# A hybrid decoder layer on one core: expert tiles in source order, and an overflow job's work in one place

## The chip, the cores and the metric

The kernel runs on 1 core of one Trainium2 chip. The metric is the device time of one execution in microseconds; the kernel before took 1674.36 us (median of 3 runs, 1674.21 to 1675.78).

## What is computed

One layer of a decoder with 1024 tokens of width 1024, in float32: a gated recurrence and an attention branch are merged into x, and then a mixture of experts is added. The change touches only the experts. Cut to that:

```python
def hier_moe(u, wg, bg, we, be, w1, w3, w2):          # 1024 tokens, 64 experts
    g_sel = argmax(u @ wg + bg)                       # one of 8 groups
    e_in_group = (u @ we + be)[group g_sel]           # 8 logits
    top_p, top_j = top_k(softmax(e_in_group), 2)      # two experts of that group
    gate = g_prob[g_sel] * top_p / sum(top_p)
    # each expert, on the tokens that chose it:
    h = silu(xb @ w1[e]) * (xb @ w3[e])               # 1024 -> 256
    y += gate * (h @ w2[e])                           # 256 -> 1024
x = x + hier_moe(rmsnorm(x), ...)
```

All 64 experts have tokens, so all their weights, 64 x 3 MiB, must pass through the core once.

## The kernel before

The first 1100 us compute projections, recurrence, attention and the merge; the change leaves them alone. Then comes **routing**: `product(tb)` and `route(tb)` (from L983 and L1006) make, for each of 8 blocks of 128 tokens, the merged x, write it to `xs_d` and to `out` in DRAM, choose the experts and give each of a token's two choices a place in a table in DRAM, `tab_d`, by an indirect transfer (L1154). A place belongs to a tile and a row: **32 tiles**, each of 128 rows, 64 rows for each of two experts. A choice that finds its expert's 64 rows full is left over and goes to a **job** of up to 64 rows of one expert. For tile 0 alone the row numbers are also made on the chip, by float32 products with a one-hot matrix (`first_tile`, L977), so that its rows can be fetched before the table is read back.

Then the **expert stage**. Its weights come in chunks of 1 MiB (`wchunk`, L1209): for a tile two chunks each of w1, w3 and w2 (`load`, L1272), six in all. There are `NW` = 19 chunk buffers, used in turn: five named c, four m (free from 973 us on) and ten w (free at 1095 us). All loads are issued by SP, in order, so a load whose buffer is still being read holds all loads behind it. For tile t the steps are

- `gather(t)`: GpSimd fetches the tile's rows from `xs_d` by an indirect DMA (L956) into one of six row tiles,
- `select(t)`: TensorE transposes the rows (L1263), VectorE scales them into xT (L1264),
- `gemm1(t)`: 64 products with w1 and w3 into ph (L1306); ScalarE and VectorE make hs of it (L1296, L1297),
- `turn(t)`: two transposes of hs (L1319), ScalarE copies them to hT (L1321),
- `gemm2(t)`: 16 products with w2 into py (L1333); VectorE adds them to the rows of `out` (L1336), which `gather_out(t)` has fetched into the same row tile (also L956),
- `scatter(t)`: GpSimd writes the rows back to `out` (L1253).

The loop (from L1471) writes gather(t+2), gather_out(t), the loads of tile t+2, gemm1(t), select(t+1), turn(t-1), gemm2(t-1), scatter(t-1). That order of the source is only a starting point: a scheduler sets the order on each engine by its own estimate. The job's rows are counted on the chip (`job_table`, `job_rec`), its chunks are loaded in the turn of tile `JI` = 6, its products (`job_run`: L1440, L1448, L1459) are split over the turns of tiles 8, 9 and 10, and its rows are fetched from `out` (L1416), added to (L1462) and written back (L1418). A loop at the end runs further jobs if there are any; in this execution there are none.

Of the kernel before, what the change touches and what calls it, by code (L numbers as in the profile page):

```python
# [38 lines left out]
NW = 19  # L39
# [4 lines left out]
JI = 6  # L44
# [7 lines left out]
def block_kernel(ctx, tc, x, positions, norm1_g, w_in, conv_w, conv_b, lru_wa, lru_ba, lru_wx,  # L52
# [878 lines left out]
    rec_0 = rt.tile([128, 4], F32, name="rec_0")  # L931
    tok_0 = rt.tile([128, 2], I32, name="tok_0")
    nc.gpsimd.memset(rec_0, 0.0)
    nc.gpsimd.memset(rec_0[:, 0:1], BIG)
    nc.gpsimd.memset(rec_0[:, 3:4], BIG)
    tokb = rt.tile([128, NB], F32, name="tokb")

    iota0 = rt.tile([128, 128], F32, name="iota0")
    nc.gpsimd.iota(iota0, pattern=[[NT_, 128]], base=0, channel_multiplier=0,
# [5 lines left out]
    nc.gpsimd.tensor_scalar(tokb, tokid, BIG, None, op0=ALU.add)  # L945
    nc.sync.dma_start(tab_d.rearrange("(p a) c -> p (a c)", p=128),
# [4 lines left out]
    nc.gpsimd.dma_start(g2c, norm2_g.rearrange("(k p) -> p k", p=128))  # L951
    blk = {}

    def rows_in(xg, at, src=xs_d):

        return nc.gpsimd.indirect_dma_start(  # L956
            out=xg, out_offset=None, in_=src,
            in_offset=bass.IndirectOffsetOnAxis(ap=at, axis=0),
            bounds_check=S - 1, oob_is_err=False)

    with pool_of(name="xe", bufs=1, side="right") as xe, \
# [15 lines left out]
        def first_tile(oh0, rec):  # L977

            for j in range(2):
                nc.tensor.matmul(pks[:, 128:132], oh0[:, j], rec[:, j], start=j == 0, stop=j == 1)  # L980
            nc.vector.tensor_tensor(rec_0, rec_0, pks[:, 128:132], op=ALU.add)
# [23 lines left out]
        def route(tb):  # L1005
            xt, ms, px = blk.pop(tb)  # L1006
            tsl = slice(tb * 128, tb * 128 + 128)
            if tb == NB - 1:
                blk["warm"] = xps.tile([128, D], F32, name="px")
                blk["xg"] = xgp.tile([128, D], F32, name="x2")  # L1010
                nc.gpsimd.memset(blk["xg"], 0.0)
# [80 lines left out]
            if tb:  # L1092
# [28 lines left out]
            oh0 = rp.tile([128, 2, 128], F32, name="oh0")  # L1121
            nc.vector.tensor_tensor(oh0, iota0[:, None, :].to_broadcast([128, 2, 128]),
                                    ps_[:, :, None].to_broadcast([128, 2, 128]), op=ALU.is_equal)
# [7 lines left out]
            rec0 = rp.tile([128, 2, 4], F32, name="rec0")  # L1131
            for c in (0, 3):
                nc.vector.tensor_scalar(rec0[:, :, c], rec[:, :, c], -BIG, None, op0=ALU.add)
# [6 lines left out]
            nc.vector.tensor_copy(rec0[:, :, 1:3], rec[:, :, 1:3])  # L1140
            if tb == NB - 1:
# [3 lines left out]
                warm(30, oh64)  # L1145
            blk["late"] = oh0, rec0
            if tb == 0:
                nc.vector.tensor_copy(acc, oh64)
            else:
                nc.vector.tensor_tensor(acc, acc, oh64, op=ALU.add)  # L1150
            for j in range(2):
# [7 lines left out]
                blk["tab"].append(sc)  # L1159

# [9 lines left out]
        for _ in route(NB - 1):  # L1170
# [9 lines left out]
    eg = open_pool(name="eg", bufs=1)  # L1180
    eh = open_pool(name="eh", bufs=2)
# [5 lines left out]
    onef = eg.tile([128, 64], F32, name="onef")  # L1187
    nc.gpsimd.memset(onef, 1.0)
    rec_all = eg.tile([128, NT_, 4], F32, name="rec_all")
    nc.gpsimd.dma_start(rec_all.rearrange("p a c -> p (a c)"),  # L1190
                      tab_d.rearrange("(p a) c -> p (a c)", p=128))
# [11 lines left out]
    def rec_of(t, c):  # L1203
        return rec_0[:, c:c + 1] if t == 0 else rec_all[:, t, c:c + 1]

    def tok_of(t, j=0):
        return tok_0[:, j:j + 1] if t == 0 else toki[:, j, t:t + 1]
# [11 lines left out]
    ring = {}  # L1219

    def rows_(kind):
        i = ring[kind] = ring.get(kind, -1) + 1
        if kind == "T":
            return xgp.tile([128, D], F32, name=f"x{3 + i % 2}")
# [326 lines left out]
```

## Time and profile before

| what | value |
|---|---|
| median of 3 runs | 1674.36 us |
| the profiled execution's own time | 1673.48 us |
| its span, first to last instruction | 1671.8 us |
| mean granted TensorE clock | 0.972 |
| TensorE busy | 1500.5 us, 90% |
| VectorE, ScalarE, GpSimd busy | 722.5, 498.8, 468.8 us |
| HBM read, written | 307.74 MB, 48.59 MB |

The page cuts the span into 40 slices of 41.8 us and gives each engine's busy share in tenths, the granted clock of TensorE, the busy share of the 16 DMA engines and the rate. The windows do the same for stretches that one chooses. A wait is put down to what ended it. PE is TensorE, DVE VectorE, ACT ScalarE, POOL GpSimd, SP the queue that issues the weight loads.

### The profile page before, as it was taken

The page shows a single profiled execution, that of the slowest core. Times are in us where ns is not written, and L with a number is a line of the kernel's source. Part 1 is how long each engine was busy: PE and PEld are TensorE (multiplying, and loading weights), DVE is VectorE, ACT ScalarE, POOL GpSimd, SP SyncE. Part 2 cuts the span into 40 slices and gives each one's busy share as a digit, 9 for nine tenths or more (in the row PEclk, how much of TensorE's full clock was granted, in tenths as well). Part 3 has the DMA queues.
Part 4 walks back from the last instruction along what each step waited for, and adds up shares of the span by engine and source line. Part 5 has one row for each costly group of instructions (what it writes and reads, how often), then busy time and mean ns, then how long its engine had stood idle before and what let it go on. Part 6 is the DMA issues. An engine that isn't in the chain of part 4 may idle for free. (4 is left out here: it accounts for less than half of the span.)

```text
span 1671.8 us, 22382 instructions
## 1 busy us (share of the span) xinstructions
PE 1500.5 (90%) x8484; PEld 1145.1 (68%) x8484; DVE 722.5 (43%) x1863; ACT 498.8 (30%) x1088; POOL 468.8 (28%) x467
## 2 busy tenths in 40 slices
PE   5999998999999989999898999979698698878876
PEld 5978886788888878888787877866354355444443
DVE  7744646320001687777885346754121122112111
ACT  5225464631111376666663112210000000000000
POOL 4034343322212245252703421132221212211100
PEclk9999999999999999999999999979899899999999
DMA  5212222353245110110206673387996999999995
GB/s 192 64 51 66 59 65 63 99 191 101 90 150 173 64 39 17 35 39 10 76 32 205 199 264 134 132 313 311 417 417 253 398 418 417 417 414 413 413 412 219
DMA packets 129665, 327.72 MB, mean 196 GB/s; under 512 B 17367, under 2 KB 82337, under 8 KB 105108
## 3 DMA queue, kind: packets, MB, share of 16 engines
q1 hardware_dynamic: 111684, 295.57, 47.3%
q0 software_dynamic: 14848, 21.46, 3.6%
q10 hardware_dynamic: 3024, 9.24, 1.4%
q8 instruction: 68, 1.11, 0.3%
q14 instruction: 41, 0.34, 0.1%
HBM read 307.74 MB, written 48.59 MB: 213 GB/s over the span
## 5 line engine op out<-in xcount | busy, mean ns | idle before, releaser
L116 POOL TENSOR_TENSOR w_lo<-w_raw,w_hi 128x1024 fp32r<-128x1024 f32 x40 | 97.8, 2444 | 263.0 <-ACT w_hi L113 263.0
L259 PE MATMUL pp<-uTh,w_hi 128*128 128x512 f32 x496 | 156.2, 396 | 1.1 <-ACT xp L368 1.1
L1264 DVE TENSOR_TENSOR x<-c,g2col 128x512 f32<-128x512 f32 (+1 forms) x66 | 44.3, 677 | 258.8 <-PE ph L1306 232.7
L262 PE MATMUL pp<-uTl,w_hi 128*128 128x512 f32 x496 | 156.1, 395 | 0.0
L1306 PE MATMUL ph<-w,x 128*64 128x256 f32 x992 | 138.9, 394 | 19.0 <-DMA w<-in_exp_w_dram 19.0
L265 PE MATMUL pp<-uTh,w_lo 128*128 128x512 f32 x496 | 155.7, 395 | 0.0
L1296 ACT ACTIVATE hs<-ph,rec_all 128x256 f32<-128x256 f32 x31 | 14.7, 473 | 440.0 <-PE ph L1306 440.0
L1306 PEld LDWEIGHTS ph<-w,x 128*64 128x64 f32 x992 | 83.6, 141 | 64.7 <-DMA w<-in_exp_w_dram 25.1
L259 PEld LDWEIGHTS pp<-uTh,w_hi 128*128 128x128 f32 x496 | 93.5, 189 | 23.3 <-ACT xp L368 1.1
L262 PEld LDWEIGHTS pp<-uTl,w_hi 128*128 128x128 f32 x496 | 93.6, 189 | 22.3
L265 PEld LDWEIGHTS pp<-uTh,w_lo 128*128 128x128 f32 x496 | 93.4, 188 | 22.1
L1002 PE MATMUL px<-wo,ms 128*128 128x512 f32 x384 | 95.0, 398 | 1.0 <-DVE ms L116 1.0
L1306 PE MATMUL ph<-c,x 128*64 128x256 f32 x592 | 85.2, 392 | 7.2 <-DMA c<-in_exp_w_dram 7.2
L113 ACT ACTIVATE w_hi<-w_raw 128x1024 fp32r<-128x1024 f32 x40 | 42.1, 1053 | 139.2 <-PE pp L262 112.8
L1002 PEld LDWEIGHTS px<-wo,ms 128*128 128x128 f32 x384 | 70.1, 188 | 16.9 <-issue 1.7
L1333 PE MATMUL py<-w,hT 128*64 128x512 f32 x280 | 76.3, 638 | 2.8 <-ACT hT L1321 1.6
L1306 PE MATMUL ph<-m,x 128*64 128x256 f32 x464 | 72.4, 394 | 6.3 <-DMA m<-in_exp_w_dram 6.3
L116 DVE TENSOR_TENSOR cTl<-gt,cTh 128x1024 fp32r<-128x1024 f32 x4 | 4.9, 1225 | 165.0 <-ACT cTh L113 165.0
L1306 PEld LDWEIGHTS ph<-c,x 128*64 128x64 f32 x592 | 50.6, 141 | 33.9 <-DMA c<-in_exp_w_dram 10.8
L1263 PE MATMUL c<-ident,o 128*128 128x128 f32 (+1 forms) x136 | 27.3, 311 | 40.1 <-DMA o<-xs_d,toki 27.0
L1263 PEld LDWEIGHTS c<-ident,o 128*128 128x128 f32 (+1 forms) x136 | 18.7, 194 | 60.7 <-issue 39.0
L1306 PEld LDWEIGHTS ph<-m,x 128*64 128x64 f32 x464 | 43.0, 142 | 24.7 <-DMA m<-in_exp_w_dram 7.6
(655 smaller groups left out, 3437.7 us busy)
## 6 DMA issues: line engine op xcount, KB each, us to landing
w<-in_exp_w_dram SPq DMA_DIRECT2D x100, 1024.0 KB
c<-in_exp_w_dram SPq DMA_DIRECT2D x51, 1024.0 KB
m<-in_exp_w_dram SPq DMA_DIRECT2D x40, 1024.0 KB
w_raw<-in_w_in_dram SPq DMA_DIRECT2D x32, 512.0 KB
xt<-in_x_dram SPq DMA_DIRECT2D x8, 512.0 KB
hg_d<-hh SPq DMA_DIRECT2D x8, 512.0 KB
gt<-hg_d SPq DMA_DIRECT2D x8, 512.0 KB
sgb_d<-gt SPq DMA_DIRECT2D x8, 512.0 KB
```

What stands on the lines that cost most here:

```text
L113: nc.scalar.activation(dst, src, AF.Copy)
L116: eng.tensor_tensor(dst, src, f32v(hi), op=ALU.subtract)
L259: nc.tensor.matmul(ps[:, s_], wh[:, k], ah[:, k, s_], start=k == 0, stop=False)
L262: nc.tensor.matmul(ps[:, s_], wh[:, k], al[:, k, s_], start=False, stop=False)
L265: nc.tensor.matmul(ps[:, s_], wl[:, k], ah[:, k, s_], start=False, stop=k == KD - 1)
L1002: nc.tensor.matmul(px[:, s_], ms[:, a, k], wos[k][:, b, s_], start=k == 0 and a + b == 0, stop=k == KD - 1 and a == 1)
L1263: nc.tensor.transpose(pt[:, kk, 0:n], x_r[:, hf * 4 + kk], ident[0:n, 0:n])
L1264: nc.vector.tensor_tensor(xT[:, hf * 4:hf * 4 + 4, 0:n], pt[:, :, 0:n], g2col[:, hf * 4:hf * 4 + 4, None].to_broadcast([128, 4, n]), op=AL ...
L1296: nc.scalar.activation(hs, ph[:, 0:256], AF.Silu, scale=rst)
L1306: nc.tensor.matmul(ph[64 * j:64 * j + 64, wi * 256:wi * 256 + 256], xT[:, k, 64 * j:64 * j + 64], w[2 * wi + j][:, k * 256:k * 256 + 256], ...
L1333: nc.tensor.matmul(py[64 * j:64 * j + 64], hT[:, kk, 64 * j:64 * j + 64], w2[j][:, o_:o_ + 512], start=kk == 0, stop=kk == 1)
```

## The change

- `pe()` stamps the tiles' transposes and products, `pin()` the row transfers with a token; instructions with the same token keep the order of the source on their engine.
- gemm1 is split in its two halves and `turn(t-1)` stands between them. gemm2(0) follows gemm1(0) at once; from tile 1 on gemm2(t-1) stands behind gemm1(t) and select(t+1), the last one too.
- The row numbers of tiles 0 and 1 are made on the chip by bf16 products with a one-hot matrix of 256 columns, from a token number in two parts, a count and a flag; gates and scales come from the table.
- Five row tiles in place of six, work space put into other tiles, and `NW` = 20 chunks.
- The job's chunks are loaded in the turn of tile 12. Its first products stand at the start of tile 14's turn, its last ones at the start of tile 15's; its row transfers and the addition follow scatter(14), and gather_out(15) follows them.
- `after()` writes orders between transfers of `out` by hand: gather_out(t) after scatter(t-4), the job's fetch after the last four scatters, gather_out(15) to (18) after the job's write, and the tail loop's two memsets after the last four scatters.

```diff
-NW = 19
+NW = 20
-JI = 6
+JI = 12
...
+    def pin(i):
+        tc.stamp_issue_order_token(i.ins, "rows")
+        return i
+    def pe(i):
+        tc.stamp_issue_order_token(i.ins, "tiles")
+    def after(i, others):
+        for o in others:
+            tc.add_manual_dep(i.ins, o.ins.name, ...)
...
+    def rows_(kind):
+        i = ring[kind] = ring.get(kind, -1) + 1
...
+        nm = ("x2", "x0", "o0", "o1", "x1")[i % 5]
...
-            for j in range(2):
-                nc.tensor.matmul(pks[:, 128:132], oh0[:, j], rec[:, j], start=j == 0, stop=j == 1)
+            for t in range(2):
+                for j in range(2):
+                    nc.tensor.matmul(pks[:, 128 + 4 * t:132 + 4 * t],
+                                     oh0[:, j, t * 128:t * 128 + 128], rec[:, j], ...)
...
-                first_tile(oh0, rec0)
-                blk["tok"] = nc.vector.tensor_copy(tok_0, rec_0[:, 0:4:3])
-                blk["g0"] = rows_in(blk["xg"], tok_0[:, 0:1])
+                first_tile(oh0, rec0)
+                nc.vector.tensor_tensor(rec_0[:, :, 0], rec_0[:, :, 0], rec_0[:, :, 1], op=ALU.add)
+                nc.vector.tensor_scalar(rec_0[:, :, 2:4], rec_0[:, :, 2:4], -BIG, BIG, ...)
+                blk["tok"] = nc.vector.tensor_tensor(tok_0, rec_0[:, :, 2:4], ...)
+                for t in range(2):
+                    rows_in(blk["xg"][t], tok_0[:, t, 0:1])
...
     def gather_out(t):
-        with tc.issue_after(st["g", min(t + 2, NT_ - 1)].ins):
-            unordered(rows_in(st["xg", t], tok_of(t, 1), out), t)
+        g = rows_in(st["xg", t], tok_of(t, 1), out)
+        unordered(g, t)
+        after(g, [stored[t - 4]] if t > 3 else [])
+        if JR <= t < JR + 4:
+            after(g, jmoves[1:])
...
-            nc.vector.scalar_tensor_tensor(jo[:, s_], py[0:64], rec[:, 1:2], jo[:, s_], ...)
-        job_move(ji, jo, False)
+            nc.vector.tensor_scalar(jx[:, s_], py[0:64], rec[:, 1:2], None, op0=ALU.mult)
         yield
+        jo = rows("xo" if rows != rows_ else "x")[0:64]
+        g = job_move(ji, jo, True, pin_)
+        nc.vector.tensor_tensor(jo, jo, jx, op=ALU.add)
+        s = job_move(ji, jo, False, pin_)
+        yield g, s
...
-        gather_out(t)
+        if t != JR:
+            gather_out(t)
...
-        gemm1(t)
+        gemm1(t, 0)
+        if t > 1:
+            turn(t - 1)
+        gemm1(t, 1)
         if t + 1 < NT_:
             select(t + 1)
-        if t:
-            turn(t - 1)
-            gemm2(t - 1)
-            scatter(t - 1)
-        if t == JI + 4:
-            next(job)
+        if t == 0:
+            turn(0)
+        if t != 1:
+            gemm2(max(t - 1, 0))
+            scatter(max(t - 1, 0))
+        if t == JR:
+            jmoves.extend(next(job))
+            after(jmoves[0], stored[-4:])
+            gather_out(t)
...
-        jbt = {n: jb.tile([128, D], F32, name="j" + n) for n in ("x", "T")}
-        nc.gpsimd.memset(jbt["x"], 0.0)
+        jbt = {n: jb.tile([128, D], F32, name="j" + n) for n in ("x", "T", "xo")}
+        for n in ("x", "xo"):
+            after(nc.gpsimd.memset(jbt[n], 0.0), stored[-4:])
```

`JR` is `JI + 3` = 15. The change moves instructions at three places that matter for what follows.

TensorE at the start of the expert stage, before: ph of x_10851 is gemm1(1), py with c_10766 and m_10768 is gemm2(0), whose chunks are the last two of tile 0.

```order
L1306 MATMUL ph<-w_10776,x_10851 64x256
L1263 MATMUL c<-ident,o_10807 128x128 x5
L1402 MATMUL c<-jrecs,kro 64x4 x4
L1263 MATMUL c<-ident,o_10807 128x128 x3
L1319 MATMUL pt<-ident,hs 128x128 x2
L1402 MATMUL c<-jrecs,kro 64x4 x4
L1333 MATMUL py<-c_10766,hT 64x512
L1402 MATMUL c<-jrecs,kro 64x4 x4
L1333 MATMUL py<-m_10768,hT 64x512
```

The same place now (gemm2 is L1368, gemm1 L1339, the tile's chunks c_10776 and m_10778):

```order
L1368 MATMUL py<-c_10776,hT 64x512
L1368 MATMUL py<-m_10778,hT 64x512
L1368 MATMUL py<-c_10776,hT 64x512
L1368 MATMUL py<-m_10778,hT 64x512
L1339 MATMUL ph<-m_10780,x_10861 64x256
L1339 MATMUL ph<-m_10782,x_10861 64x256
```

gemm2(0) stood behind the whole of gemm1(1); now it stands ahead of its first product.

TensorE at the job's last products, before: x_11788 is tile 10, L1459 the job's products with its w2 chunk, w_11432.

```order
L1333 MATMUL py<-c_11534,hT 64x512
L1333 MATMUL py<-m_11536,hT 64x512
L1263 MATMUL c<-ident,o_11923 128x128
L1459 MATMUL py<-w_11432,jhT 64x512
L1306 MATMUL ph<-m_11614,x_11788 64x256
L1459 MATMUL py<-w_11432,jhT 64x512 x3
L1306 MATMUL ph<-m_11616,x_11788 64x256
```

Now (L1491, chunk m_11969; c_11876 and c_11878 are tile 13's w2, x_12237 is tile 15):

```order
L1368 MATMUL py<-c_11876,hT 64x512
L1368 MATMUL py<-c_11878,hT 64x512
L1491 MATMUL py<-m_11969,hT 64x512 x4
L1339 MATMUL ph<-w_12063,x_12237 64x256
L1339 MATMUL ph<-w_12065,x_12237 64x256
```

The products with the job's w2 chunk now run one turn after its first products (L1475, ahead of gemm1(14)), right behind gemm2(13), whose chunks were loaded just before the job's.

GpSimd, a tile in the middle before (o_11821 is tile 12, o_12363 tile 18, x_12187 tile 16, o_11923 tile 13):

```order
L1253 DMA out_dram<-o_11821,toki 1024x1024
L956 DMA o_12363<-xs_d,toki 128x1024
L956 DMA x_12187<-out_dram,toki 128x1024
L1253 DMA out_dram<-o_11923,toki 1024x1024
```

And now, at the job's transfers (x_11949 is tile 14, x_12056 tile 15, o_12144 tile 16, o_12265 tile 17, x_12374 tile 18, x_12363 the job's):

```order
L976 DMA o_12265<-xs_d,toki 128x1024
L1284 DMA out_dram<-x_11949,toki 1024x1024
L1452 DMA x_12363<-out_dram,ji 64x1024
L1452 DMA out_dram<-x_12363,ji 1024x1024
L976 DMA x_12056<-out_dram,toki 128x1024
L976 DMA x_12374<-xs_d,toki 128x1024
L976 DMA o_12144<-out_dram,toki 128x1024
L1284 DMA out_dram<-x_12056,toki 1024x1024
```

Before, a gather reached six tiles ahead and stood behind the scatter of the tile whose row tile it takes; now it reaches three tiles past the last scatter, and the job's fetch and write stand in line between scatter(14) and the transfers of tiles 15, 18 and 16.

## Rows read from the trace of the kernel before

**Rows 1.** The page's slices: DMA share in tenths and rate of each fortieth.

```profile
DMA  5212222353245110110206673387996999999995
GB/s 192 64 51 66 59 65 63 99 191 101 90 150 173 64 39 17 35 39 10 76 32 205 199 264 134 132 313 311 417 417 253 398 418 417 417 414 413 413 412 219
```

**Rows 2.** Windows of the expert stage, us from the span's start.

```profile
core 0: us, PE busy (x) PEld busy (x) DVE busy (x) ACT busy (x) POOL busy (x), PEclk, DMA share, GB/s
1096.00:1126.00 30.00, 18.85 (x151) 16.06 (x151) 16.23 (x91) 4.00 (x9) 10.09 (x12) 0.72 1.00 391
1126.00:1131.00 5.00, 5.00 (x50) 3.26 (x48) 0.00 (x0) 0.00 (x0) 3.78 (x5) 1.00 0.58 177
...
1141.00:1152.00 11.00, 10.07 (x82) 6.98 (x83) 5.81 (x16) 0.86 (x2) 1.61 (x2) 1.00 0.26 77
...
1272.00:1298.00 26.00, 24.48 (x144) 12.46 (x146) 4.68 (x7) 0.86 (x2) 4.28 (x5) 0.93 0.34 122
1298.00:1630.00 332.00, 267.37 (x1748) 148.46 (x1745) 62.53 (x99) 16.74 (x39) 59.48 (x59) 0.95 1.02 415
1630.00:1656.00 26.00, 22.17 (x158) 13.79 (x160) 4.36 (x7) 1.24 (x3) 2.90 (x3) 1.00 0.86 327
```

**Rows 3.** DMA queues from 1352 to 1628 us: packets, MB, share of 16 engines.

```profile
q1 hardware_dynamic: 14016, 102.05, 89.6%
```

**Rows 4.** Waits of SP's queue, 1080 to 1672 us: total us, times, longest.

```profile
SPq L1277 <- PE py L1333: 52.8, 11, 16.1
SPq L1277 <- PE py L1459: 33.6, 1, 33.6
```

**Rows 5.** Timeline of SP's load issues: start, us from first to last, what.

```profile
1128.35 21.67 SPq L1277 DMA_DIRECT2D c<-in_exp_w_dram  x5
...
1210.60 3.31 SPq L1427 DMA_DIRECT2D w<-in_exp_w_dram  x3
```

**Rows 6.** Timeline, start of the stage: start us, us, what, [idle before <-releaser].

```profile
1113.08 1.26 POOL L956 DMA_INDIRECT x<-xs_d,tok  x1 [0.96 <-issue]
1123.78 8.00 PE L1306 MATMUL ph<-c,x 128*64 128x256 f32 x64
1125.44 1.06 POOL L956 DMA_INDIRECT o<-xs_d,toki  x1 [5.32 <-DVE toki L1194]
1159.03 3.65 PE L1333 MATMUL py<-w,hT 128*64 128x512 f32 x16
```

**Rows 7.** Timeline of one tile in the steady part (half of gemm1 in the third).

```profile
1376.25 3.70 PE L1333 MATMUL py<-w,hT 128*64 128x512 f32 x16
1379.44 1.02 POOL L956 DMA_INDIRECT o<-xs_d,toki  x1 [11.01 <-DMA out_dram<-o,toki]
1380.41 3.67 PE L1306 MATMUL ph<-w,x 128*64 128x256 f32 x32
1388.36 0.71 PE L1263 MATMUL c<-ident,o 128*128 128x128 f32 x4 [0.82 <-DVE x L1264]
```

**Rows 8.** The job in the timeline, then landing times of lines L956 and L1253.

```profile
1249.57 6.64 PE L1440 MATMUL ph<-w,x 128*64 128x256 f32 x30
1303.72 1.40 DVE L1462 SCALAR_TENSOR_TENSOR o<-py,jrec,o 64x512 f32<-64x512 f32 x2 [11.35 <-DMA o<-out_dram,ji]
...
DMA to landing us min/median/max: 2.1/9.2/12.6
DMA to landing us min/median/max: 8.4/10.0/13.6
```

**Rows 9.** Timeline of the end of the span.

```profile
1650.21 0.97 POOL L1512 MEMSET jx<- 128x1024 f32 x1
1655.21 1.94 PE L1306 MATMUL ph<-c,x 128*64 128x256 f32 x14 [0.43 <-DMA c<-in_exp_w_dram]
1658.23 0.51 PE L1319 MATMUL pt<-ident,hs 128*128 128x128 f32 x2 [1.08 <-DVE hs L1297]
```

More of the change, by code (lines that the diff above doesn't have):

```diff
@@ L977, in first_tile @@
         def first_tile(oh0, rec):
[L979 to L981 removed]
+            for t in range(2):
+                for j in range(2):
+                    nc.tensor.matmul(pks[:, 128 + 4 * t:132 + 4 * t],
+                                     oh0[:, j, t * 128:t * 128 + 128], rec[:, j], start=j == 0,
+                                     stop=j == 1)
+            r_ = rec_0.rearrange("p t c -> p (t c)")
+            nc.vector.tensor_tensor(r_, r_, pks[:, 128:136], op=ALU.add)
         def product(tb, half):
@@ L1009, in route @@
                 blk["warm"] = xps.tile([128, D], F32, name="px")
-                blk["xg"] = xgp.tile([128, D], F32, name="x2")
-                nc.gpsimd.memset(blk["xg"], 0.0)
+                blk["xg"] = [rows_("x") for t in range(2)]
             def warm(n, lhsT):
@@ L1130, in route @@
                                         op=ALU.min)
-            rec0 = rp.tile([128, 2, 4], F32, name="rec0")
-            for c in (0, 3):
-                nc.vector.tensor_scalar(rec0[:, :, c], rec[:, :, c], -BIG, None, op0=ALU.add)
+            rec0 = rp.tile([128, 2, 4], BF16, name="rec0")
+            nc.vector.tensor_copy(rec0[:, :, 0:3], tokc[:, tb][:, None, :].to_broadcast([128, 2, 3]))
+            nc.vector.tensor_scalar(rec0[:, :, 3], rec[:, :, 3], BIG, None, op0=ALU.is_lt)
             den = rp.tile([128, 1], F32, name="den")
@@ L1297, in gated, with gemm1 @@
         nc.vector.scalar_tensor_tensor(hs, ph[:, 256:512], rst, hs, op0=ALU.mult, op1=ALU.mult)
-    def gemm1(t):
-        xT = st.pop(("xT", t))
+    def gemm1(t, wi):
+        xT = st["xT", t]
         w = st["w", t]
-        ph = hps.tile([128, 512], F32, name="ph")
-        for wi in range(2):
-            for k in range(KD):
-                for j in range(2):
-                    nc.tensor.matmul(
-                        ph[64 * j:64 * j + 64, wi * 256:wi * 256 + 256],
-                        xT[:, k, 64 * j:64 * j + 64],
-                        w[2 * wi + j][:, k * 256:k * 256 + 256], start=k == 0,
-                        stop=k == KD - 1)
+        if wi == 0:
+            st["ph", t] = hps.tile([128, 512], F32, name="ph")
+        ph = st["ph", t]
+        for k in range(KD):
+            for j in range(2):
+                pe(nc.tensor.matmul(
+                    ph[64 * j:64 * j + 64, wi * 256:wi * 256 + 256],
+                    xT[:, k, 64 * j:64 * j + 64],
+                    w[2 * wi + j][:, k * 256:k * 256 + 256], start=k == 0,
+                    stop=k == KD - 1))
+        if wi == 0:
+            return
         hs = eh.tile([128, 256], F32, name="hs")
@@ L1461, in job_run @@
             s_ = slice(hf * 512, hf * 512 + 512)
-            nc.vector.scalar_tensor_tensor(jo[:, s_], py[0:64], rec[:, 1:2], jo[:, s_],
-                                           op0=ALU.mult, op1=ALU.add)
-        job_move(ji, jo, False)
+            nc.vector.tensor_scalar(jx[:, s_], py[0:64], rec[:, 1:2], None, op0=ALU.mult)
         yield
-    st["xg", 0] = blk["xg"]
-    gather(1)
+        jo = rows("xo" if rows != rows_ else "x")[0:64]
+        pin_ = pin if rows == rows_ else lambda i: i
+        g = job_move(ji, jo, True, pin_)
+        nc.vector.tensor_tensor(jo, jo, jx, op=ALU.add)
+        s = job_move(ji, jo, False, pin_)
+        yield g, s
+    for t in range(2):
+        st["xg", t] = blk["xg"][t]
     for t in range(3):
```

141 lines of the change are left out of this document (73 added, 68 removed).

## The prediction

> **What bounds the kernel now.** I read the page's slices first, then the windows of the expert stage, then who holds the load queue back, then single instructions of that stage. In the slices [rows 1] the DMA line stands at 9 almost without a break over the last third of the span; before that no stage fills it. So the end is set by the stage that streams the expert weights. Its rate is 415 GB/s with a DMA share of 1.02 from 1298 to 1630 us [rows 2], and there TensorE is busy 267 of 332 us: the transfers are the limit, TensorE has some room. In the steady part 102.05 MB pass on the load queue in 276 us [rows 3]; a chunk has 1.0486 MB, so a chunk costs 276 / 97.3 = **2.84 us**, the row transfers beside it included, and a tile of six chunks 17.0 us. Of itself a chunk takes 1.0486 MB / 415 GB/s = 2.53 us.
>
> A stage that is limited by transfers can be shortened in three ways only: fewer bytes (the change keeps them all), fewer holes in the stream, or less work behind the last byte. The windows show the holes [rows 2]. From 1126 to 1131 the rate is 177 GB/s: 5 x (1 - 177/415) = 2.9 us idle. From 1141 to 1152 it is 77: 11 x (1 - 77/415) = 9.0 us. From 1272 to 1298 it is 122: 26 x (1 - 122/415) = 18.4 us. Together **30.3 us**. Who makes them is in the waits of the load queue [rows 4]: one wait of 16.1 us and one of 33.6 us on products py, the second on the job's own (L1459), the longest of that list. SP issues its loads in order, so a chunk whose old content is not yet used up holds all loads behind it.
>
> **The change, part by part.** I number tiles from 0, and chunks in load order.
>
> *The job in one place (third hole).* Before, the job's three chunks are issued from 1210.60 [rows 5], but its last products stand in TensorE's order only between gemm2 of tile 9 and gemm1 of tile 10, and the chunk stays taken till then; the load that wants it 19 chunks later waits 33.6 us, of which the loads already issued cover all but 18.4. Now its first products run at the start of tile 14's turn, its last ones before tile 15's first product: it gives its chunks back between those of tiles 13 and 15, in the order in which they were loaded. The hole should go whole: **-18.4 us**; the other bound is 0, if the same wait shows up at the new place. What covers the job's longer TensorE work: 6.64 us for its first products [rows 8] plus about 5 for the rest, against three chunks' loads, 8.5 us, and the room of 17.0 - 13 us that each tile leaves.
>
> *gemm2(0) ahead of gemm1(1), and a 20th chunk (first two holes).* The gather of tile 0 is issued at 1113.08 [rows 6]; the chain of small VectorE instructions ahead of it gets a few longer and its products shorter, and I take it as unmoved (within 1 us to either side, the size of the idle time in front of it). So gemm1(0) still runs 1123.8 to 1131.8 [rows 6]. The 20th chunk puts 2.5 us of transfer into the first hole: 2.9 - 2.5 = 0.4 left. Then the fifth chunk of tile 0 comes free with gemm2(0): 1131.8, tile 1's transposes 1.4, the counts and hT some 3, the products 3.7 [rows 7] give 1139.7, where before the issue of the fifth c stood at 1128.35 + 21.67 = 1150.0 [rows 5]. The four chunks reissued at 1128 keep the engines busy to about 1141, so with 2 us from issue to data (an estimate: the shortest landing of a row gather is 2.1 [rows 8]) 0.7 us of idle remains. That tile 1's rows are gathered with tile 0's, not from 1125.44 [rows 6], is what lets TensorE go on without waiting. But now a third gap opens. The two w2 chunks of tile 1 come free only with gemm2(1), which the new order puts behind gemm1(2) and the transposes of tile 3: gemm1(1) with the job's counting between its halves to 1150, then 1.4 + 7.9 + 1.4 + 3.7 gives 1164 (before, it ended at 1159.03 + 3.65 = 1162.7 [rows 6]). Six chunks are free until then, 6 x 2.84 = 17.0 us from 1141.7 to 1158.7; data flow again at 1166: 7.3 us. So 0.4 + 0.7 + 7.3 = 8.4 us remain of 11.9: **-3.5 us**. Bounds: 0, if the start slips by as much, and -11.9, if TensorE is quicker than this sum.
>
> *Row transfers in source order, five row tiles in place of six.* Before, each gather stands right behind the scatter that frees its tile and GpSimd waits some 11 us for it [rows 7]. Now a gather needs a scatter issued a whole tile earlier, so the wait goes; a gather is issued a tile and a half (about 25 us) before its transposes, and lands in 9.2 us at the median, 12.6 at most [rows 8]. No gain and no loss: neither is on the path while the stream is full. If that cover went, a late gather would stop TensorE, not yet the loads.
>
> *The job's rows at tile 15.* The pinned order gives GpSimd a chain: scatter(14) must land (10.0), the job's gather (9.2), VectorE's addition (1.4 for as many elements [rows 8]), the job's scatter (10.0), and only then gather_out(15) and gather(18), which land 10 us later: some 41 us after scatter(14). Queued behind it are gather(18), gather_out(16) and scatter(15) on GpSimd and, on VectorE, hs of tile 16 and all evacuations. TensorE wants gather(18) after about 27 us, so it falls some 14 us behind, 16 with the four gathers that then again follow their scatter. This costs nothing as long as loads find free chunks: of 20 about 8 are held at the normal pace (the tile in work and the w2 before it), and 12 x 2.84 = 34 us of loads are ahead. I take **0**; the upper bound, with every landing at its longest, is a lag of about 32 us, just inside.
>
> *The end.* Before, gemm2(30) ran ahead of gemm1(31). Now it stands between gemm1(31) and the last turn: 3.7 us where only 1.08 us of waiting stood [rows 7, 9]: **+2.6 us** behind the last weights. Two memsets of the tail loop's tiles now wait for the last scatters, where one ran at 1650.21, covered [rows 9]: 2 x 0.97 = **+1.9 us** (from 0, if the drain behind them is waiting anyway, to 3).
>
> In these last products the granted clock was 1.00, its upper level, with TensorE busy 22.17 of 26 us [rows 2]; by that row they cost what they cost before, and the sum stands. The Trainium skill (TensorE: Matmul & The Clock Gate, HAM oscillation) says that short batches of products between waits for DMA fall back to the lower level again and again. By that rule the last products, 1.94 + 3.7 + 0.5 + 3.7 = 9.8 us, would take twice that and the kernel 9.8 us more than my sum.
>
> **The sum.** -18.4 - 3.5 + 2.6 + 1.9 = -17.4 us, against the profiled execution's own 1673.48 us (span 1671.8 and 1.7 around it): **1656.1 us**. The median of the runs shown, 1674.36, is 0.9 us above it; that is noise beside the sum.
>
> **The rivals.**
> 1. *The start does not gain, or loses.* The third gap grows: gemm2(1) late by waits of the job's counting on VectorE, whose chain now also holds an addition of tile 0. For it: TensorE has that counting in the middle of gemm1(1). Against it: the pieces are short. Time 1660 to 1668.
> 2. *The job's chain makes a hole of its own.* Place: GpSimd between scatter(14) and gather(18). It decides once TensorE's lag passes 34 us; at 42 us the time is 1664. For it: three landings in a row in one queue, and chunks of VectorE work held behind. Against it: the reserve above.
> 3. *The clock falls and TensorE becomes the bound: slower than before.* In stretches with waits the granted clock averages 0.93 to 0.95 [rows 2], so some of them are already spent at the lower level. A tile's products, 7.3 + 3.7 + 1.4 + 0.5 = 12.9 us, would take 25.8 there, 8.8 us over the tile's 17.0. After four such tiles in a row the reserve of 34 us is gone; the kernel is slower than before once six follow each other (6 x 8.8 = 53 > 34 + 17.4); at eight it is 1656.1 + 36 = 1692. Against it: an engine that falls behind stops waiting, and from 1126 to 1131, busy throughout, the clock is back at 1.00 after a stretch with a mean of 0.72 [rows 2]. The Trainium skill's rule just cited speaks for this case.
> 4. *The change moves the wait and does not remove it.* The loads at the new place wait as long as at the old: 1674, no change.
> 5. *Both early holes go.* 1656.1 - 8.4 = 1648, less if the memsets hide.
>
> **How the numbers follow.** The forecast has 55 in 100, rival 1 15, rival 2 12 (one of them within the band of no change), rival 3 6, rival 4 4, rival 5 8. A measurement here can tell 0.2%, 3.3 us, from nothing: faster 55 + 15 + 11 + 8 = 0.89, same 0.05, slower 0.06. The range goes from rival 5 with the tail at its lower bound, 1647, to rivals 1 and 2 with a hole of some 13 us, 1669; outside lie rivals 3 and 4 and the edges of the others.
>
> **What would show it.** The windows of the changed kernel should be at about 415 GB/s from 1166 to the last chunk, with no dip around tiles 14 to 18; no wait of the load queue on the job's py of more than a few us; before 1166 short dips that add to about 8 us; gemm2(30) between gemm1(31) and the last transposes; two memsets behind the last scatter. A dip below 300 GB/s after tile 15 would make the step on the job's rows wrong; a DMA share under 1 with TensorE busy throughout, and a granted clock near 0.5, would make rival 3 right.

## The result, and the profile after

The changed kernel took **1660.91 us** (median of 4 runs, 1659.31 to 1662.71), the kernel before beside it 1674.28: a ratio of 0.9922, interval 0.9904 to 0.9939, or 13.4 us less. The forecast was 1656.1 in a range of 1647 to 1669. The same kernel measured once more in a later group (below) took 1658.34 beside 1675.33, a ratio of 0.9896 [0.9881, 0.9911], 17.0 us less, where the sum had said 17.4 against one profiled execution.

The page's slices of the changed kernel, DMA share and rate, to be held against [rows 1]:

```profile
DMA  6212221262345210101215655369999999999994
GB/s 193 58 47 65 58 75 55 69 224 88 102 143 171 89 39 14 36 14 36 76 33 171 221 191 197 134 244 392 364 416 418 418 419 417 414 400 411 416 405 162
```

The slice at 253 GB/s, the job's hole, is gone. What remains below 410 in the expert stage is two slices at its start (392, 364), two late ones (400, 405) and the last (162), in which the stream ends. The windows show it closer; the columns are those of [rows 2]:

```profile
1132.00:1152.00 20.00, 19.32 (x200) 12.40 (x197) 11.15 (x24) 0.86 (x2) 7.00 (x7) 1.00 0.95 365
1162.00:1170.00 8.00, 8.00 (x58) 4.23 (x56) 3.18 (x5) 0.47 (x1) 1.50 (x2) 1.00 0.45 154
...
1272.00:1298.00 26.00, 20.90 (x132) 10.68 (x130) 5.17 (x8) 0.86 (x2) 6.07 (x6) 0.93 1.02 419
1298.00:1440.00 142.00, 117.34 (x736) 65.29 (x734) 27.88 (x44) 7.62 (x18) 22.10 (x22) 0.92 1.02 417
1440.00:1530.00 90.00, 76.21 (x482) 41.35 (x480) 17.50 (x27) 4.29 (x10) 20.16 (x20) 0.93 1.02 406
1618.00:1638.00 20.00, 18.71 (x132) 11.12 (x130) 3.18 (x5) 1.24 (x3) 2.04 (x2) 0.95 0.84 307
```

At 1272 the rate is 419. Between 1126 and 1132, where the first gap stood before, it is 414. The early gaps that are left are 20 x (1 - 365/415) = 2.4 us and 8 x (1 - 154/415) = 5.0 us, 7.4 where [rows 2] had 11.9. From 1440 to 1530 the rate is 2% below the stream's own, with the DMA share as high as ever.

Of the waits of the load queue [rows 4], the one on the job's py (33.6 us) is gone, and of the others the longest on a second product is 13.7:

```profile
SPq L1309 <- PE py L1368: 37.6, 5, 13.7
```

One cut makes the runs comparable. The last load that SP issues ahead of the experts writes the empty table (L946, now L950). It starts at 973.38 us in the profile of before and at 979.04 in that of the changed kernel, with the same order of TensorE's work ahead of it:

```profile
979.04 0.32 SPq L950 DMA_DIRECT2D tab_d<-tin  x1
...
1099.33 1.73 SPq L1309 DMA_DIRECT2D w<-in_exp_w_dram  x2
```

Over all fourteen profiles of this study that start lies between 973.4 and 980.2, in no order of kernels. So I cut each profiled execution at five points that its timeline shows: the table's write, the first load into a w chunk, the end of gemm1(31), the issue of the last scatter, the end of the span. All in us:

| profile | table's start | to first w load | to end of gemm1(31) | to last scatter | to the end | from table to end |
|---|---|---|---|---|---|---|
| before | 973.38 | 122.0 | 561.7 | 6.9 | 7.8 | 698.4 |
| changed | 979.04 | 120.3 | 541.6 | 9.2 | 10.8 | 681.9 |
| changed, again | 975.20 | 119.9 | 542.2 | 9.2 | 10.6 | 681.8 |
| before, job in one place | 974.27 | 120.9 | 547.3 | 7.5 | 7.8 | 683.5 |
| 19 chunks | 980.15 | 120.0 | 545.2 | 9.1 | 10.5 | 684.9 |
| gemm2(1) early | 975.44 | 120.3 | 537.7 | 9.2 | 10.9 | 678.1 |
| job's chunks held | 974.96 | 120.1 | 545.2 | 9.2 | 10.5 | 684.9 |
| gemm2(30) ahead | 976.42 | 119.9 | 544.1 | 8.6 | 10.5 | 683.1 |
| short clearings | 974.28 | 119.9 | 542.2 | 9.2 | 10.7 | 681.9 |
| last four tiles early | 974.75 | 119.8 | 542.8 | 6.9 | 10.5 | 680.0 |
| wait inside the loop | 973.47 | 120.4 | 541.5 | 9.2 | 7.8 | 678.8 |
| rows not pinned | 974.06 | 120.5 | 544.0 | 9.2 | 10.5 | 684.1 |
| three edits, tiles 0 to 2 | 976.02 | 119.9 | 541.0 | 6.9 | 7.9 | 675.7 |
| three edits, tiles 0 and 1 | 978.26 | 120.2 | 538.7 | 6.9 | 7.8 | 673.5 |

Two executions of the changed kernel that differ by 3.9 us in their spans differ by 0.1 in the last column. The time to the end of gemm1(31) is 541.5 to 542.2 in the four executions whose expert loop is that of the changed kernel (changed, again, short clearings, wait inside the loop), so a difference of 0.7 there says nothing. What follows goes by these columns, with the medians beside them. Each row is one execution, and against the kernel before the medians differ from the last column by up to 3.3 us (13.4 for 16.5 less in the first group, 21.6 for 24.9 in the last row): a step of two or three us rests on the table, not on the medians. The first two rows show where the time went: 20.1 us less in the stream, 1.7 less in front of it, 2.3 and 3.0 more behind it: 16.5 in all.

### The profile page after: what moved, and what is told of

It reads as the page before. It is cut to its first block, busy times and chain, and to the rows that moved or that the text cites. A ratio compares the mean times of both kernels' runs of the same rounds, so it can differ in the third digit from the quotient of the medians.

```text
span 1660.9 us, 22272 instructions
## 1 busy us (share of the span) xinstructions
PE 1508.6 (91%) x8484; PEld 1141.0 (69%) x8484; DVE 723.9 (44%) x1859; ACT 499.1 (30%) x1088; POOL 470.6 (28%) x467
## 5 line engine op out<-in xcount | busy, mean ns | idle before, releaser
L1339 PE MATMUL ph<-w,x 128*64 128x256 f32 x1104 | 163.1, 405 | 26.3 <-DMA w<-in_exp_w_dram 24.0
L1339 PEld LDWEIGHTS ph<-w,x 128*64 128x64 f32 x1104 | 94.7, 145 | 84.3 <-DMA w<-in_exp_w_dram 26.2
L1329 DVE SCALAR_TENSOR_TENSOR hs<-ph,rec_all,hs 128x256 f32<-128x256 f32 x32 | 15.4, 482 | 289.0 <-ACT hs L1328 289.0
L1356 ACT ACTIVATE hT<-pt 128x256 f32<-128x256 f32 x32 | 12.3, 384 | 343.0 <-PE pt L1354 343.0
L1339 PE MATMUL ph<-c,x 128*64 128x256 f32 x512 | 81.3, 413 | 13.0 <-DMA c<-in_exp_w_dram 12.9
L1038 PEld LDWEIGHTS px<-wo,ms 128*128 128x128 f32 x384 | 70.2, 189 | 17.5 <-issue 1.8
L1339 PE MATMUL ph<-m,x 128*64 128x256 f32 x432 | 68.0, 414 | 14.0 <-DMA m<-in_exp_w_dram 10.9
L1339 PEld LDWEIGHTS ph<-c,x 128*64 128x64 f32 x512 | 47.5, 149 | 44.2 <-DMA c<-in_exp_w_dram 15.2
L1368 PE MATMUL py<-w,hT 128*64 128x512 f32 x288 | 71.1, 611 | 0.5 <-ACT hT L1356 0.5
L1339 PEld LDWEIGHTS ph<-m,x 128*64 128x64 f32 x432 | 39.0, 149 | 36.1 <-DMA m<-in_exp_w_dram 9.3
L897 PE MATMUL pp<-c,w 128*128 128x512 f32 x240 | 56.9, 392 | 0.0
L120 PE MATMUL tp<-ptl,vh 128*128 128x256 f32 (+1 forms) x160 | 47.8, 299 | 9.7 <-DVE ptl L116 9.3
```

The costliest lines, as they stand in the source:

```text
L120: nc.tensor.matmul(ps, lh, rl, start=False, stop=False)
L897: nc.tensor.matmul(pb[:, s_], w[:, a, k], oT[k][b][:, s_], start=k == 0 and a + b == 0, stop=k == KD - 1 and a == 1)
L1038: nc.tensor.matmul(px[:, s_], ms[:, a, k], wos[k][:, b, s_], start=k == 0 and a + b == 0, stop=k == KD - 1 and a == 1)
L1329: nc.vector.scalar_tensor_tensor(hs, ph[:, 256:512], rst, hs, op0=ALU.mult, op1=ALU.mult)
L1339: pe(nc.tensor.matmul(ph[64 * j:64 * j + 64, wi * 256:wi * 256 + 256], xT[:, k, 64 * j:64 * j + 64], w[2 * wi + j][:, k * 256:k * 256 + 25 ...
L1356: nc.scalar.activation(hT, pt, AF.Copy)
```

## The experiments

Each was timed in five rounds beside the kernel before, in three groups and a single last run.

**The changed kernel again.** No edit.

> The changed kernel once more, unaltered. Its profiled execution wrote the empty table (L950, the last load issue ahead of the experts) at 979.0 us, before it was 973.4; TensorE's order up to there is the same. Theory: these some 4 us belong to that one execution, so they vary: here L950 stands anywhere between 973 and 979, and the median is 1659 to 1662. Rival: the change lengthens the phases ahead of the experts; then L950 is at 979 again within 1 us, whatever the execution.

Median 1658.34; the table's write started at 975.20. The theory holds: the phases ahead of the experts vary from execution to execution by more than most terms of the sum.

**The kernel before, with the job in one place and nothing else.**

```diff
         if t in (JI + 2, JI + 3):
             next(job)
+        if t == JI + 3:
+            next(job)
...
-        if t == JI + 4:
-            next(job)
```

> The kernel before with one edit: the job's last products run one turn earlier, right behind its transposes. Theory (the job's chunk is held too long): the hole of 18.4 us around 1272 to 1298 goes whole, 1674.3 - 18.4 = 1656, and the windows there read about 415 GB/s. Rival (the wait only moves): a wait of the load queue of some 30 us stands at the new place, 1674. Second rival (TensorE or the row transfers take part of it back): 1660 to 1668.

Median 1659.87, 15.5 us less than before; from table to end 14.9 less. So this one edit brings nine tenths of what the whole change gains in the end; of the 20.1 us that the change takes out of the stream it brings 14.4, while behind the stream the change loses 5.3 and this edit 0.6. The stretch of the hole and the one behind it, then two rows of TensorE's and GpSimd's timelines:

```profile
1272.00:1302.00 30.00, 13.49 (x96) 7.96 (x96) 4.78 (x9) 1.24 (x3) 7.01 (x7) 0.80 1.01 417
1302.00:1312.00 10.00, 9.80 (x50) 4.48 (x52) 1.50 (x2) 0.00 (x0) 1.02 (x1) 0.75 0.77 294
...
1302.20 0.45 PE L1263 MATMUL c<-ident,o 128*128 128x128 f32 x1 [13.93 <-DMA o<-xs_d,toki]
...
1293.67 1.03 POOL L956 DMA_INDIRECT o<-xs_d,toki  x1 [10.65 <-DMA out_dram<-o,toki]
```

The hole is gone whole (417 where [rows 2] have 122), but a new one of 10 x (1 - 294/415) = 2.9 us follows. TensorE had waited 13.9 us for the rows of a tile whose gather GpSimd issued late, behind the landing of a scatter. The granted clock averages 0.80 and 0.75 in these two stretches, so products at its lower level may have a part in the new hole. That is the second rival, and the changed kernel does not have this hole.

**19 chunks.**

```diff
-NW = 20
+NW = 19
```

> The changed kernel with 19 chunks in place of 20. Theory: the early gaps end when tile 1's second product gives its chunks back, and one chunk less is loaded by then: 2.8 us more than the changed kernel beside it (about 1663.7), all of it before 1175 us. Rival 1 (the 20th chunk covers the later part of the stage, where TensorE falls behind at the job): over 5 us more, with a dip after 1400. Rival 2 (no value): no change.

Median 1661.26, 2.9 more than the changed kernel in the same group; 3.0 from table to end. The early windows carry it, and no dip stands behind them:

```profile
1132.00:1140.00 8.00, 8.00 (x89) 5.49 (x86) 1.09 (x2) 0.67 (x2) 1.92 (x2) 0.92 0.64 216
1162.00:1174.00 12.00, 12.00 (x92) 6.75 (x90) 3.18 (x5) 0.86 (x2) 3.03 (x3) 1.00 0.56 202
1174.00:1440.00 266.00, 228.88 (x1512) 126.91 (x1510) 54.85 (x86) 14.45 (x34) 49.37 (x49) 0.96 1.02 417
```

The theory's 2.8 is met: a chunk more is worth one chunk's time, once, at the start.

**gemm2(1) early.**

```diff
-        if t > 1:
+        if t > 2:
             turn(t - 1)
         gemm1(t, 1)
...
-        if t == 0:
-            turn(0)
-        if t != 1:
-            gemm2(max(t - 1, 0))
-            scatter(max(t - 1, 0))
+        if t < 2:
+            turn(t)
+        if t != 2:
+            gemm2(t if t < 2 else t - 1)
+            scatter(t if t < 2 else t - 1)
```

> The changed kernel with gemm2(1) right behind gemm1(1), select(2) and turn(1), as it does tile 0, in place of behind gemm1(2). Theory (the gap of 5.0 us around 1162 to 1170 is the wait for tile 1's w2 chunks): it goes, about 5 us less than the changed kernel beside it (1656). Rival 1 (the next chunks, tile 2's, are then late by the same): no change, with a gap a tile later. Rival 2 (TensorE waits for hs and hT, 2 us, and everything behind is late): 1 to 3 us less only.

Median 1655.04, 3.3 less than the changed kernel beside it; 3.7 from table to end. The window of the third gap, first of the changed kernel again, then of this one:

```profile
1158.00:1166.00 8.00, 8.00 (x58) 4.27 (x56) 3.18 (x5) 0.47 (x1) 1.31 (x2) 1.00 0.40 129
```

```profile
1158.00:1166.00 8.00, 7.37 (x68) 4.92 (x66) 1.68 (x3) 0.47 (x1) 6.00 (x6) 1.00 1.01 407
1166.00:1182.00 16.00, 16.00 (x126) 9.23 (x124) 3.18 (x5) 1.24 (x3) 3.03 (x3) 1.00 0.90 351
```

The gap was the wait for tile 1's w2 chunks. Half of it moves on: 16 x (1 - 351/415) = 2.5 us stand a tile later, part of which rival 1 had.

**The job's chunks held two turns longer.** They are loaded in turn 10; products and rows stay.

```diff
             wts.append(t)
+        yield
         jx = rows("x")[0:64]
...
-        if t == JI:
+        if t in (JI - 2, JI):
             next(job)
```

> The changed kernel with the job's three chunks loaded two turns earlier (turn 10), its products and rows where they are. Theory (a hole is the time a chunk is held past its turn in the ring, less what the loads already issued cover): the chunks are wanted again 12 chunks, 34 us, earlier; in the changed kernel the last of them came free 9.6 us before it was wanted (products end 1356.8, reissue about 1366.4), so the load queue waits some 24.5 us; before, a wait of 33.6 made a hole of 18.4, 15.2 covered, so the hole is 9 us, and the time about 9 us above the changed kernel (1659 median of its runs, so 1668). Rival 1 (what counts is only that the products stand together): no change. Rival 2 (nothing covers the wait now): 24 us more.

Median 1661.63; 3.1 more than the changed kernel from table to end, not 9. The hole itself is there, 30 x (1 - 308/415) = 7.7 us:

```profile
1330.00:1360.00 30.00, 25.00 (x145) 13.95 (x146) 6.36 (x11) 1.60 (x4) 5.07 (x5) 0.98 0.79 308
1440.00:1530.00 90.00, 75.91 (x505) 41.16 (x506) 19.37 (x30) 4.31 (x11) 20.22 (x20) 0.96 1.02 416
```

```profile
SPq L1309 <- PE ph L1476: 16.3, 2, 13.2
SPq L1309 <- PE py L1492: 15.3, 1, 15.3
```

The load queue waits 13.2 us on the job's first products and 15.3 on its last, 28.5 where I had 24.5 for the last chunk alone, and the hole is 7.7 for 9. So a chunk held past its turn does make a hole. Its size came near the forecast partly by luck: by the same sum, a wait less 15.2 us covered, 28.5 us would have made 13.3, and some 21 were covered. What the loads in flight cover is no fixed amount. More than half of the hole is given back later: where the changed kernel runs at 406 GB/s (1440 to 1530), this one runs at 416, 2.2 us of the difference, and from 1530 to 1615 at 415 and 416 where the changed kernel again runs at 412 and 405, another 0.9. Why is open (see the last section).

**gemm2(30) ahead of gemm1(31).**

```diff
+        if t == NT_ - 1:
+            turn(t - 1)
+            gemm2(t - 1)
+            scatter(t - 1)
         gemm1(t, 0)
-        if t > 1:
+        if 1 < t < NT_ - 1:
             turn(t - 1)
...
-        if t != 1:
+        if t != 1 and t < NT_ - 1:
             gemm2(max(t - 1, 0))
```

> The changed kernel with turn(30) and gemm2(30) ahead of gemm1(31) instead of behind it. As predicted for the change (gemm2(30) behind the last weights costs 2.6): about 2.5 us less. Rival, by the trace of the changed kernel: TensorE has hardly waited for data since tile 30's first product (0.2 to 1.3 us after 1617), so it is late itself, and moving work within its last 25 us gains nothing: 0, with gemm1(31) starting 4 us later and ending behind the landing of its last weights.

Median 1660.03; 1.2 more than the changed kernel from table to end. The rival is right. TensorE's timeline of the end, the changed kernel first:

```profile
1639.03 1.73 PE L1339 MATMUL ph<-w,x 128*64 128x256 f32 x13 [0.16 <-DMA w<-in_exp_w_dram]
...
1640.80 3.60 PE L1368 MATMUL py<-m,hT 128*64 128x512 f32 x15
1644.33 0.50 PE L1354 MATMUL pt<-ident,hs 128*128 128x128 f32 x2
1645.37 3.65 PE L1368 MATMUL py<-w,hT 128*64 128x512 f32 x16 [0.53 <-ACT hT L1356]
```

```profile
1629.85 3.65 PE L1368 MATMUL py<-m,hT 128*64 128x512 f32 x16 [0.53 <-ACT hT L1356]
1633.33 7.08 PE L1339 MATMUL ph<-w,x 128*64 128x256 f32 x64
1641.53 0.50 PE L1354 MATMUL pt<-ident,hs 128*128 128x128 f32 x2 [1.12 <-DVE hs L1329]
1642.57 5.35 PE L1368 MATMUL py<-w,hT 128*64 128x512 f32 x16 [0.53 <-ACT hT L1356]
```

With gemm2(30) ahead, all 64 products of gemm1(31) run without one wait for data: TensorE is the late one, and changing the order within its last turn does not help it. The last products took 5.35 us here for 3.65, at a granted clock of 0.72:

```profile
1642.00:1648.00 6.00, 5.39 (x17) 1.44 (x16) 0.76 (x2) 0.38 (x1) 0.00 (x0) 0.72 0.00 1
```

Those 1.7 us are the clock's and not the order's. At 3.65 this version would stand some 0.5 us below the changed kernel, which is still not the 2.5 of the theory.

**The last four tiles early.** The loop's lag of one second product is given up at tile 28.

```diff
-        if t > 1:
+        if 1 < t <= 28:
             turn(t - 1)
...
-        if t == 0:
-            turn(0)
-        if t != 1:
-            gemm2(max(t - 1, 0))
-            scatter(max(t - 1, 0))
+        if 1 < t <= 28:
+            gemm2(t - 1)
+            scatter(t - 1)
+        if t < 1 or t >= 28:
+            turn(t)
+            gemm2(t)
+            scatter(t)
...
-    turn(NT_ - 1)
-    gemm2(NT_ - 1)
-    scatter(NT_ - 1)
```

> The changed kernel with gemm2(t) right behind gemm1(t) for tiles 28 to 31 (27 and 28 follow each other in turn 28), so that TensorE carries no product of an earlier tile into the last one. Theory (TensorE's lag of one second product at the end is what the tail costs): gemm1(31) ends with its last weights and only its own second product follows: 2 to 2.5 us less. Rival (the wait of turn and hT, about 1.6 us a tile, takes it back, or the last bytes set the end): 0 to 1 us less.

Median 1657.11; 1.9 less from table to end. TensorE waits for the last weights again, and nothing of tile 30 is left behind them:

```profile
1635.37 1.94 PE L1339 MATMUL ph<-w,x 128*64 128x256 f32 x14 [1.32 <-DMA w<-in_exp_w_dram]
1638.40 0.50 PE L1354 MATMUL pt<-ident,hs 128*128 128x128 f32 x2 [1.09 <-DVE hs L1329]
1639.44 3.65 PE L1368 MATMUL py<-w,hT 128*64 128x512 f32 x16 [0.53 <-ACT hT L1356]
```

From gemm1(31) to the last scatter it takes 6.9 us as before, not 9.2; gemm1(31) itself ends 0.6 to 1.2 later.

**Short clearings in the tail.**

```diff
         for n in ("x", "xo"):
-            after(nc.gpsimd.memset(jbt[n], 0.0), stored[-4:])
+            nc.gpsimd.memset(jbt[n][:, 8:D], 0.0)
+            after(nc.gpsimd.memset(jbt[n][:, 0:8], 0.0), stored[-4:])
```

> The changed kernel with the tail loop's two clearings cut in two: 1016 columns of each that wait for no scatter, and 8 columns that do. Theory: from the issue of the last scatter to the end takes 10.8 us, before 7.8; the clearings behind its landing are the difference, and 1.7 to 3.0 us go. Rival (the end is set by the landing and what follows it on the other engines): no change.

Median 1657.51; from table to end the same, 681.9, and still 10.7 us behind the last scatter's issue. GpSimd's timeline:

```profile
1645.55 0.97 POOL L1284 DMA_INDIRECT out_dram<-o,toki  x1 [2.71 <-DVEq L1559]
1646.52 0.96 POOL L1556 MEMSET jxo<- 128x1016 f32 x1
1649.14 0.10 POOL L1557 MEMSET jx<- 128x8 f32 x1 [1.67 <-issue]
```

The clearing of 1016 columns is covered and the short one takes 0.10 us, but it cannot start before 1649.14, 3.6 us after the scatter's issue. So the work is not what costs; that the wait is, the next run tests.

**The same wait, moved into the loop.**

```diff
         for n in ("x", "xo"):
-            after(nc.gpsimd.memset(jbt[n], 0.0), stored[-4:])
+            nc.gpsimd.memset(jbt[n], 0.0)
...
         g = job_move(ji, jo, True, pin_)
+        if rows != rows_:
+            after(g, stored[-4:])
```

> The changed kernel with the wait for the last four scatters taken from the two clearings and put on the job's fetch inside the tail loop, which runs no turn here. Theory (cutting the clearings down changed nothing, so it is the wait for the last scatter's landing that now stands ahead of the closing steps on GpSimd): from the last scatter's issue to the end 7.8 us again, not 10.6, 2.8 us less. Rival (the end waits for that landing elsewhere too): no change.

Median 1654.74; 3.0 less from table to end, and 7.8 us from the last scatter to the end, as before:

```profile
1644.55 0.97 POOL L1284 DMA_INDIRECT out_dram<-o,toki  x1 [2.70 <-DVEq L1560]
1645.51 0.97 POOL L1558 MEMSET jxo<- 128x1024 f32 x1
```

The clearing follows the issue at once (1645.51). By the source, the reading of the job count and the branch of the tail loop stand next in line; that they now run beside the scatter's landing is the reading that fits the 2.8 us, the profile does not show these steps.

**Row transfers not pinned.**

```diff
     def pin(i):
-        tc.stamp_issue_order_token(i.ins, "rows")
         return i
```

> The changed kernel with the order of GpSimd's row transfers left to the scheduler again (TensorE's order stays as it is). As predicted for the change (the order of row transfers is worth 0): no change, 1657 to 1660. Rival (from the kernel before with the job in one place, where TensorE waited 13.9 us for a row gather that stood behind a scatter, and the stream lost 2.9 us): about 3 us more, with a wait of TensorE on rows near the job's transfers.

Median 1658.79; from table to end 2.3 more. It is neither of the two: no loss at the job, but one at the start of the stage. GpSimd's timeline there:

```profile
1102.10 0.97 POOL L1177 DMA_INDIRECT tab_d<-rec,pos  x1 [0.30 <-DVE rs_t L106]
1113.14 0.95 POOL L987 MEMSET x<- 128x1024 f32 x1 [10.07 <-DMA out_dram<-x]
1114.25 1.24 POOL L1177 DMA_INDIRECT tab_d<-rec,pos  x1 [0.16 <-DVE kro L1381]
...
1117.07 1.06 POOL L975 DMA_INDIRECT x<-xs_d,tok  x1 [0.30 <-issue]
```

The scheduler puts the clearing of a row tile, which waits 10.1 us for a write to `out`, ahead of the last two table writes. The first gather then starts 22.5 us after the first w load, not 18.1 as in the changed kernel again. Of the 2.3 us, 1.8 stand in the stream and 0.6 in front of the first w load. From 1126 to 1172 the gaps are 22 x (1 - 328/415) + 24 x (1 - 310/415) = 10.7 us, in the changed kernel again 20 x (1 - 368/415) + 8 x (1 - 129/415) = 7.8.

**Three edits together:** tiles 0 to 2 early (in the loop above, `t < 3`), the last four early, the wait in the loop.

> The changed kernel with three edits together: gemm2(t) right behind gemm1(t) for tiles 0, 1 and 2 and again for 28 to 31, and the wait of the tail moved into the loop. If the gains add: 3.8 (tiles 0 and 1, by the profiles) and up to 2.4 for tile 2, 1.9 and 2.8, so 8.5 to 10.9 us less than the changed kernel, about 1649. Rival (they hide one another, since an earlier stream finds TensorE later): 5 us less or fewer.

Median 1652.17; 6.1 less than the changed kernel from table to end, not 8.5. The tail's two gains are whole (6.9 and 7.9). Against the run with the last four tiles early, the time to the end of gemm1(31) fell by 1.8, not 3.7.

**The same with tiles 0 and 1.**

> The three edits again, but with tiles 0 and 1 alone at the start, as in the run that gained 3.8 us. If tile 2's early product was what took the gain back (the gap only moved to 1190), the time from the empty table's write to the end is 681.8 - 3.8 - 1.9 - 2.8 = 673.3 us. Rival (the loss came with the last four tiles, whose data landed 0.9 us later): 675 to 676, as with three tiles.

From table to end **673.5**, where 673.3 was expected; median 1652.87, a ratio to before of 0.9862 [0.9843, 0.9881]. By the table the three gains add, 8.3 us beyond the changed kernel, and leaving tile 2's early product out ends gemm1(31) 2.3 us sooner (538.7 for 541.0). This is the best of the versions by the table. The medians do not confirm the last step: beside the kernel before, both versions are 21.6 us faster. That tile 2's early product took the third gain back is thus shown by one execution each.

## Why the prediction was right, point by point

**The job in one place, -18.4: right.** Alone it took 14.9 us from the kernel before, 14.4 of them in the stream, where 18.4 of hole less 2.9 of a new one make 15.5. Rival 4, the wait that only moves, is out: from 1360 to 1620 the load queue waits on its own earlier loads, and 0.5 us in all on TensorE:

```profile
SPq L1309 <- PE pt L1354: 0.5, 2, 0.3
```

The other direction is tested too: held two turns longer, the job's chunks make a hole again (7.7 us), though only 3.1 us of time.

**The early gaps, -3.5: measured 11.9 - 7.4 = 4.5.** The third gap came where the sum put it, behind gemm2(1), with 5.0 us for 7.3; what was left of the first two is 2.4 for 1.1. So the sum is right to 1.0 because two errors in it point opposite ways. The 20th chunk is worth 3.0 by its removal, and placing gemm2(1) earlier takes the gap away there, half of it to come back a tile later. The first gather was unmoved within half a microsecond: 17.7 us after the first w load before, 17.5 and 18.1 after. Neither rival 1, a grown third gap, nor rival 5, no gap, came.

**The row transfers, 0: right in the steady part, incomplete at the start.** Their fixed order is worth 2.3 us in one execution, and the trace shows the loss at the start, where a waiting clearing gets in front of the first gather; no run moves that clearing alone. (A gather now stands four tiles past the last scatter, gather(17) behind scatter(13), not three as said above.) I had costed only the transfers in a row and not the clearings that share GpSimd's queue with them.

**The job's rows at tile 15, 0: right.** The chain in GpSimd's timeline of the changed kernel:

```profile
1370.40 1.00 POOL L1284 DMA_INDIRECT out_dram<-x,toki  x1 [6.34 <-DVE x L1371]
1380.02 0.96 POOL L1452 DMA_INDIRECT x<-out_dram,ji  x1 [8.61 <-DMA out_dram<-x,toki]
1387.89 0.96 POOL L1452 DMA_INDIRECT out_dram<-x,ji  x1 [6.92 <-DVE x L1499]
1394.81 1.02 POOL L976 DMA_INDIRECT x<-out_dram,toki  x1 [5.96 <-DMA out_dram<-x,ji]
1396.14 1.00 POOL L976 DMA_INDIRECT x<-xs_d,toki  x1 [0.31 <-issue]
```

```profile
1388.66 6.58 PE L1339 MATMUL ph<-m,x 128*64 128x256 f32 x32 [3.04 <-DVE x L1296]
...
1406.04 1.97 PE L1295 MATMUL c<-ident,x 128*128 128x128 f32 x8 [6.76 <-DMA x<-xs_d,toki]
```

gather(18) is issued 25.7 us after scatter(14), and I had some 31 to its issue. TensorE waited 3.0 us for VectorE and 6.8 for the rows of gather(18), then 1.6 and 2.6 for the next two gathers, 14.0 in all where I had 14 to 16 of lag, and the stream stayed at 417. Rival 2 was near all the same: in the kernel before with the job moved, where such a gather stood behind a scatter with 19 chunks and six row tiles, a wait of 13.9 us did cost 2.9.

**gemm2(30) behind the last weights, +2.6: the size was right (9.2 for 6.9, 2.3), the reason was not.** I had taken its place for the cost. Moving it alone gained nothing (0.5 us at most, with the slower clock of that run taken out), since TensorE comes into the last tile late; only without the lag from tile 28 on do 1.9 us come back.

**The two clearings, +1.9: measured 3.0, and again the reason was another.** I priced two memsets by their durations. Their work is free; the wait for the last scatter in front of the closing steps is the cost, and it goes whole once it stands where it is needed.

**Not in the sum:** 1.7 to 2.1 us less between the table's write and the first w load, of which the kernel before with the job moved shows 1.1 too, so that at most about 1 belongs to the edits in routing; and 18.4 + 4.5 - 20.1 = 2.8 us lost again later in the stream, some 2 of them from 1440 to 1530. Against 17.4 what is measured from the table to the end is 16.5 and 16.6. That it comes so near is partly luck: 1.0 and 1.7 more gained than the sum has, 0.8 and 2.8 less, almost cancel. The first median stood 4.8 us above the forecast. The profiled execution, the slowest of the four, stood 6.6 above it, and 5.7 of that are the phases ahead of the experts: its table's write was that much later than in the one of before. In the other three that part was not measured.

**The clock.** From 1618 to 1638 the granted clock averaged 0.95, from 1640 to 1650 1.00, and gemm2(31) took 3.65 us where it had taken 3.67, so rival 3 and the 9.8 us that I had put beside the sum did not come:

```profile
1640.00:1650.00 10.00, 8.49 (x42) 2.87 (x38) 3.49 (x5) 0.86 (x2) 0.99 (x1) 1.00 0.13 48
```

The Trainium skill's rule (TensorE: Matmul & The Clock Gate, HAM oscillation), that short batches between waits for DMA fall to the lower level, did not show at this place. In the run with gemm2(30) ahead the last products did run slower (5.35 us at 0.72), but the waits in front of them, 1.12 and 0.53 us, were for VectorE and ScalarE, and with nearly the same two waits (1.09 and 0.53) the run with the last four tiles early took 3.65 us. So no run here ties that fall to the waits.

## What to carry to other kernels

In a stage limited by transfers, ask of each buffer in the ring when it is wanted again and when its last reader runs; the difference, less what is already in flight, is the hole (18.4 us here before; 7.7 when it was made again, of which the time kept 3.1), and putting a side job's reads where its buffers come up in the ring can be worth more than all the reordering around it. Price an added wait by what stands behind it on its engine, and not by the duration of the instruction that carries it. Before you compare two profiles term by term, cut them at a point ahead of which the order of work is the same, since the part ahead varied here by more than most terms.

## What the runs showed of the hardware

With the same order of TensorE's instructions, the first 973 us took up to 6.8 us longer in some executions than in others (973.4 to 980.2 over fourteen profiles). The granted clock goes with it: after its first rise, TensorE stands at the lower of its two levels for 24 to 31 us of this part in the eleven executions up to 976.4, and for 34 to 38 us in the three from 978.3 on (24 in the kernel before, 34 in the changed one). TensorE is busy over 90% there, so 10 us more at half the clock are some 5 us of its work, an estimate, of the 5.7 that lie between these two. Why the clock fell more often in some executions is not shown.

The stream ran at 406 GB/s from 1440 to 1530 us in the changed kernel, at a DMA share of 1.02, and at 416 at the same share and time in the version that had lost 7.7 us to a hole earlier. I had expected a lost hole to stay lost. The queue of the loads from 1450 to 1500, first before, then changed (packets, MB, share of 16 engines):

```profile
q1 hardware_dynamic: 2564, 18.68, 90.3%
```

```profile
q1 hardware_dynamic: 2440, 17.77, 88.1%
```

Each byte took 2.6% longer. Two causes that come to mind do not fit the version that ran at 416. It moved more row data in that stretch, not less; the row transfers' queue from 1450 to 1500, changed, then that version:

```profile
q0 software_dynamic: 1644, 2.33, 12.9%
```

```profile
q0 software_dynamic: 1850, 2.78, 15.0%
```

And from tile 14 on it loads the same weights into the same chunks in the same order. Whether the pace of TensorE or the timing of the transfers against each other slows the stream was not tried; the cause is open.
